# Up projection of a hybrid encoder step: the A11·B11 product of the first four column pairs taken ahead of the sets, and all 16 pairs by seven products

## The chip, the core and the metric

One core of a Trainium2 chip runs the whole kernel as one launch. The metric is the device time in microseconds of one execution. TensorE is PE in the profile (PEld is its weight load), VectorE is DVE, ScalarE is ACT, GpSimd is POOL, and SyncE, which issues nearly all transfers, is SP.

## What is computed

The reference is one encoder layer over 1056 columns (1024 prompt frames and 32 sample frames), with D_MODEL 1024 and D_FF 4096. The change lies in the first matrix product of the MLP:

```python
x = x + merged @ w_o
f = jnp.square(jax.nn.relu(rmsnorm(x, g_ffn) @ w_up)) @ w_down
x = x + f
```

Everything is fp32. Each operand is split into a high and a low part (fp32r), and a product of two operands takes three matmuls: high·high, high·low, low·high.

## The kernel before, in words

**Stages.** Input projection, attention and convolution, output projection (`w_o`, until 769 us of the span), up projection (769 to 1101 us), down projection (1101 to 1428 us), gate and final norm. Activations are held transposed: features in partitions, the 1056 columns along the free axis, in two halves of 528 and four quarters of 264.

**Up projection.** The 32 column blocks of `w_up` are taken as 16 pairs, `u0` to `u15`. With the two blocks of a pair as rows, and even and odd k blocks as columns, a pair is a 2x2 block product: A11, A12, A21, A22 (weights) times B11, B21 (first half of the columns) and B12, B22 (second half). One "product" over a quarter is 4 k blocks x 3 matmuls of 128x264, that is 12 matmuls (`products`). Pair `u0` is made plainly (`up_plain`): 8 products over two quarters each, 192 matmuls. Pairs `u1` to `u15` are made by seven products instead of eight (`seven`), with sums of weights S1 to S4 and sums of operands T1 to T4: 168 matmuls each. Between the products, PSUM results are moved and combined: `p1` (A11·B11), `s5` and `u2` are copied to SBUF by ACT, and four combinations with them are made by DVE.

**Weights of a pair.** `fetch_up` loads the two blocks (512 KB each) into `wraw`, which has four buffers. `prepare` is a generator that makes the sums on POOL (`s3`, `a21`, `s2`, `s4`, in that order, four instructions), then splits A11 and A12 with `load_w` (a cast to `whi` by ACT and a subtraction to `wlo` by DVE, 128x1024), and S1, S2, S3, S4, A22 with `half_w` (a cast `sh` by ACT and a subtraction `sl` by DVE, 128x512). Its argument `at` says after how many steps each of these is issued. `whi` and `wlo` come from a pool with two buffers each; `sh` and `sl` have four each:

```python
wsp = ctx.enter_context(tc.tile_pool(name="wsp", bufs=2))
...
hi = wsp.tile([P, kb, P], F32R, tag="whi", name=f"whi_{name}")
lo = wsp.tile([P, kb, P], F32R, tag="wlo", name=f"wlo_{name}")
nc.scalar.copy(hi, raw)
nc.vector.tensor_tensor(lo, raw, hi.bitcast(F32), op=ALU.subtract)
```

**What sets the order.** The instructions of PE, DVE, ACT and POOL stand in each engine's queue in the order in which the code issues them. `run(body)` steps through one generator, such as `seven`, which yields after each product over a quarter, and after each step it advances every generator in the list `side` by one: `prepare` of the next pair, `all_t` (splits of T1 to T4, two instructions for each of 16 tiles), loads, and `mean_squares` (three small products and eight reciprocals on DVE). SP's transfers stand in one queue of their own.

**End of the output projection.** `wo_post` adds the last result into the residual, `operands(7)` splits B22 and B21 of the last feature block, ACT squares it (`sq7`) and DVE adds that to `ssq1`. `prepare_plain("u0", 0)` stands inside the last round, `prepare_plain("u0", 1)` behind the first matmuls of `up_plain`.

**End of a pair.** After the A22 product over the first quarter, `mid_sums` makes three sums on DVE (`ta`, `m1`, `ta`, 128x528); after the second quarter ACT takes relu and square, and DVE makes a fourth sum (`tb`). All go to DRAM for the down projection.

Of the kernel before, what the change touches and what calls it, by code (L numbers as in the profile page):

```python
# [48 lines left out]
def tile_step(  # L49
# [129 lines left out]
    def prepare(s_, at=(6, 8, 10, 12, 14, 18)):  # L179
# [17 lines left out]
        }  # L197
        parts = [partial(part, k, x) for k, x in (("S1", a21), ("S2", s2), ("S3", s3), ("S4", s4), ("A22", a22))]
        for n, g in zip(at, [first] + parts):
            steps.setdefault(n, []).append(g)  # L200
        for n in range(max(at) + 1):
            for f in steps.get(n, ()):
                f()  # L203
# [18 lines left out]
    def seven(s_, m1, m2, last, after=None):  # L222


        after = after or {}
        w = ws.pop(s_)
        p1, u2, s5 = (
            [wpool[0].tile([P, TQ], F32, tag=k, name=f"{k}_{s_}{t}") for t in range(2)] for k in ("p1", "u2", "s5")
        )
# [9 lines left out]
        for t, a, b in q:  # L239
            x[t] = product("A11", "B11", t)  # L240
            nc.scalar.copy(p1[t], x[t])
            yield
        for t, a, b in q:
            z[t] = product("S1", "T1", t)
            nc.scalar.copy(s5[t], z[t])
            yield
        for t, a, b in q:
            product("S2", "T2", t, x[t])
            nc.scalar.copy(u2[t], x[t])
            yield  # L250
        for t, a, b in q:
            dve(m1[:, a], product("A12", "B21", t), p1[t], op=add)
            yield
        done("11")
# [1062 lines left out]
    def operands(n):  # L1317

        g = gffn[:, n : n + 1]
        by_half = list(zip(halves, ("B21", "B22") if n % 2 else ("B11", "B12")))  # L1320
        for c, k in by_half[::-1] if n == KD - 1 else by_half:
            d, src = operand(k, n // 2), x1[n][:, c]
            nc.scalar.activation(d[:, 0, :], src, AF.Copy, scale=g)
# [77 lines left out]
    def output_projection():  # L1401

        for n in range(KD):
            if n + 2 < KD:
                wo_fetch(n + 2)
            else:
                fetch_up(n + 2 - KD)
            if n + 1 < KD:
                wo_high(n + 1)
            else:  # L1410
                prepare_plain("u0", 0)
            if n == 0:
                branch_post(("a", KD - 1), 2)
                for t in range(NTT):
# [66 lines left out]
    def up_plain():
        w = ws["u0"]
        m = blk("m1_0"), blk("m2_0")
        terms, p_ = ((w["A11"], "B12"), (w["A12"], "B22")), []
        for t in range(2):
            p_.append(products(f"up01{t}", terms, quarters[t], ks=range(3), last=False))
        prepare_plain("u0", 1)
        for c, i in ((1, 0), (1, 1), (0, 0), (0, 1)):
            for t in range(2):
                a, b = (("A11", "A12"), ("A21", "A22"))[i]  # L1490
                terms = ((w[a], f"B1{c + 1}"), (w[b], f"B2{c + 1}"))
                if (c, i) == (1, 0):
                    ps = products("", terms, quarters[t], p_[t], ks=[3], first=False)
# [4 lines left out]
            square(m[i], halves[c])
            if (i, c) != (0, 1):
                nc.sync.dma_start(md(f"B{i + 1}{c + 1}", 0), m[i][:, halves[c]])  # L1500
        side.append(after(3, mid_sums(0, *m)))
# [408 lines left out]
    with tc.manual_schedule(engines=MM):  # L1910
# [10 lines left out]

        for j in range(KD // 2 - 1):
            fetch_t(j, 0)
        side += [prepare("u1", AT1), all_t(), after(3, call(fetch_up, 2))]
        run(up_plain())
        x1.clear()
        side.append(after(14, mean_squares()))
        for s_ in range(1, NSET):
            if s_ + 1 < NSET:
                side.append(prepare(f"u{s_ + 1}"))  # L1930
            if s_ + 2 < NSET:
                side.append(after(5, call(fetch_up, s_ + 2)))
            if s_ == NSET - 1:
# [161 lines left out]
```

## Time and profile before

| | |
|---|---|
| median of 3 runs | 1541.33 us (1541.09 to 1541.75) |
| profiled execution | 1542.94 us, span 1541.1 us |
| PE busy | 1522.7 us (99%) |
| DVE busy | 1056.5 us (69%) |
| ACT busy | 747.3 us (48%) |
| POOL busy | 335.1 us (22%) |
| HBM read, written | 186.31 MB, 80.72 MB |
| mean granted PE clock | 0.997 |

The span runs from the first to the last recorded instruction; the profiled execution took 1.8 us more than its span. In timeline rows the columns are start, duration, engine, line, operation, output<-input, count, and in brackets the idle time before it with what ended it. A range such as 278/284/293 is the shortest, the median and the longest of a group in ns.

### The profile page before, as it was taken

To read this page: it belongs to the slowest core of one execution; us is meant where nothing else is said; L and a number is where in the kernel's file an instruction comes from. 1 tells how busy PE (TensorE), PEld (TensorE's weight loads), DVE (VectorE), ACT (ScalarE), POOL (GpSimd) and SP (SyncE) were. 2 spreads that over 40 slices of the span, in tenths; PEclk is the share of its full clock that TensorE was granted. 3 is DMA by queue.
4 is the path that set the end of the run, shared out by engine and by line. 5 is a ranking of instruction groups with operands and counts; after the bars stand their busy time and mean duration, and the time that the engine had idled before them with its cause. 6 is when DMAs were issued, how large, how long until landed. Compare 5 with 4: busy or idle time off the path is not lost. (4 is left out here: it accounts for less than half of the span.)

```text
span 1541.1 us, 29464 instructions
## 1 busy us (share of the span) xinstructions
PE 1522.7 (99%) x11840; PEld 1511.4 (98%) x11840; DVE 1056.5 (69%) x1425; ACT 747.3 (48%) x1367; POOL 335.1 (22%) x342
## 2 busy tenths in 40 slices
PE   8999999999999999999999999999999999999997
PEld 8999999999999999999999999999999999999997
DVE  7568656656777887665577555445577986789756
ACT  6544444434555664322365555555643334434654
POOL 2123322230222232101312222222020220000253
PEclk9999999999999999999999999999999999999999
DMA  6513545415644843354354343444886897683443
GB/s 221 202 53 111 192 153 193 166 45 182 197 117 151 281 141 133 133 180 176 121 188 152 140 154 137 142 148 154 290 289 199 286 326 237 210 273 122 138 129 117
DMA packets 110569, 268.96 MB, mean 175 GB/s; under 512 B 12992, under 2 KB 30144, under 8 KB 110432
## 3 DMA queue, kind: packets, MB, share of 16 engines
q1 hardware_dynamic: 110144, 266.75, 51.2%
q8 instruction: 93, 1.52, 0.4%
q14 instruction: 44, 0.36, 0.1%
q10 hardware_dynamic: 288, 0.32, 0.1%
HBM read 186.31 MB, written 80.72 MB: 173 GB/s over the span
## 5 line engine op out<-in xcount | busy, mean ns | idle before, releaser
L1690 PE MATMUL ps_dn<-fh,whi_dn 128*128 128x264 f32 x896 | 254.7, 284 | 0.0
L1691 PE MATMUL ps_dn<-fl,whi_dn 128*128 128x264 f32 x896 | 254.5, 284 | 0.0
L1692 PE MATMUL ps_dn<-fh,wlo_dn 128*128 128x264 f32 x896 | 254.5, 284 | 0.0
L1692 PEld LDWEIGHTS ps_dn<-fh,wlo_dn 128*128 128x128 f32 x896 | 168.7, 188 | 0.0
L1691 PEld LDWEIGHTS ps_dn<-fl,whi_dn 128*128 128x128 f32 x896 | 168.5, 188 | 0.0
L1690 PEld LDWEIGHTS ps_dn<-fh,whi_dn 128*128 128x128 f32 x896 | 168.5, 188 | 0.0
L809 DVE TENSOR_TENSOR_SCAN r<-r 128x128 f32<-128x128 f32 (+3 forms) x64 | 86.6, 1353 | 5.6 <-POOL r L802 5.6
L203 POOL TENSOR_TENSOR s_i<-raw_i,raw_i 128x512 f32<-128x512 f32 x30 | 41.2, 1372 | 223.7 <-DVE slS_i L166 194.0
L203 POOL TENSOR_TENSOR s_u<-raw_u,raw_u 128x512 f32<-128x512 f32 x30 | 44.1, 1471 | 184.6 <-DVE slS_u L166 184.4
L1577 ACT CAST whi_dn<-raw_dn 128x1024 fp32r<-128x1024 f32 x40 | 42.1, 1051 | 84.7 <-PE ps_dn L1691 84.7
L802 POOL TENSOR_SCALAR_AFFINE_SELECT r<-r 128x128 f32<-128x128 f32 x64 | 40.1, 627 | 192.1 <-ACT r L795 192.1
L1583 DVE TENSOR_TENSOR wlo_dn<-raw_dn,whi_dn 128x1024 fp32r<-128x1024 f32 x40 | 61.3, 1531 | 28.5 <-ACT whi_dn L1577 28.5
L1774 POOL TENSOR_TENSOR xx<-xx,pgs 128x384 f32<-128x384 f32 (+1 forms) x23 | 24.3, 1058 | 216.4 <-DVE pgs L1773 209.8
L1603 DVE TENSOR_TENSOR fl<-mr,fh 128x1056 fp32r<-128x1056 f32 x56 | 70.0, 1249 | 0.3 <-ACT q L1643 0.3
L849 DVE TENSOR_TENSOR at<-pa,at 128x512 fp32r<-128x512 f32 (+2 forms) x96 | 51.9, 550 | 24.7 <-ACT at L848 24.2
L216 PE MATMUL ps_A11u<-T,shS_u 128*128 128x264 f32 x240 | 68.4, 285 | 0.0
L218 PE MATMUL ps_A11i<-T,slS_i 128*128 128x264 f32 x240 | 68.4, 285 | 0.0
L217 PE MATMUL ps_A11u<-T,shS_u 128*128 128x264 f32 x240 | 68.3, 285 | 0.0
L216 PE MATMUL ps_A11i<-T,shS_i 128*128 128x264 f32 x240 | 68.3, 285 | 0.0
L217 PE MATMUL ps_A11i<-T,shS_i 128*128 128x264 f32 x240 | 68.2, 284 | 0.0
L218 PE MATMUL ps_A11u<-T,slS_u 128*128 128x264 f32 x240 | 68.0, 283 | 0.0
L166 DVE TENSOR_TENSOR slS_i<-s_i,shS_i 128x512 fp32r<-128x512 f32 x45 | 36.1, 806 | 45.4 <-ACT shS_i L164 45.1
(451 smaller groups left out, 5607.8 us busy)
## 6 DMA issues: line engine op xcount, KB each, us to landing
raw_dn<-in_w_down_dram SPq DMA_DIRECT2D x56, 512.0 KB, 4.6
raw_i<-in_w_in_dram SPq DMA_DIRECT2D x34, 512.0 KB, 4.5
mr<-mdT SPq DMA_DIRECT2D x32, 528.0 KB, 5.7
raw_u<-in_w_up_dram SPq DMA_DIRECT2D x32, 512.0 KB, 3.6
mdB<-m SPq DMA_DIRECT2D x48, 264.0 KB, 2.4
mr<-mdB SPq DMA_DIRECT2D x24, 528.0 KB, 6.4
raw_pg<-in_w_ple_gate_dram SPq DMA_DIRECT2D x17, 512.0 KB, 3.6
mdT<-ta SPq DMA_DIRECT2D x32, 264.0 KB, 2.1
```

The source lines that it names most:

```text
L203: f()
L216: nc.tensor.matmul(p_, wh[:, k, :], o[:, 0, c], start=new and n == 0, stop=False, **on)
L217: nc.tensor.matmul(p_, wh[:, k, :], o[:, 1, c], start=False, stop=False, **on)
L218: nc.tensor.matmul(p_, wl[:, k, :], o[:, 0, c], start=False, stop=z, **on)
L809: nc.vector.tensor_tensor_scan(rev, rev, rev, 1.0, ALU.mult, ALU.bypass)
L849: nc.vector.tensor_tensor(al, pt[:, :nb, :], ah.bitcast(F32), op=ALU.subtract)
L1577: nc.scalar.copy(hi, dws[u])
L1583: dve(lo, raw, hi.bitcast(F32), op=sub)
L1603: dve(l, mraw.pop(v), opd[v].bitcast(F32), op=sub)
L1690: nc.tensor.matmul(ps, hi[:, j, :], oh, start=j == 0, stop=False)
L1691: nc.tensor.matmul(ps, hi[:, j, :], ol, start=False, stop=False)
L1692: nc.tensor.matmul(ps, lo[:, j, :], oh, start=False, stop=j == NP_ - 1)
```

## The change

The A11·B11 product of pairs `u0` to `u3` (`P` in the code) is made first, in `up_early`, and kept in SBUF (`held_p`, tiles `pe0` and `pe2`); the A12·B21 product (`C`) is added to it in the same PSUM buffer, and relu and square of that go to DRAM as B11 of the down projection. Each early pair needs one weight block only (`early_fetch`, `early_split`; names `eu0` to `eu3`). `up_plain` is gone. All 16 pairs then run through `up_set`. For the four held ones `seven` makes five products over two quarters (S1, S2, S3, S4, A22; 120 matmuls), and DVE adds or subtracts the held `p1` where `p1` used to be left in PSUM. Both weight blocks of these pairs are loaded (again for the first block) and prepared as before, without the A11, A12 split. The first half of `m1` is read back from DRAM for the sums. B12 is no longer split, as plain pairs alone used it.

```diff
-AT1 = (5, 4, 6, 7, 8, 12)
+AT1 = (5, 4, 6, 8, 10, 12)
+NEARLY = 4
+AT2 = (4, 6, 8, 10, 12, 15)
...
-            steps.setdefault(n, []).append(g)
+            if g is not first or s_ not in held_p:
+                steps.setdefault(n, []).append(g)
...
+    def early_split(s_):
+        early_w[s_] = even_odd(load_w(None, 0, KD, f"e{s_}", raw=early_raw.pop(s_)))
+
+    def early_first(s_, t):
+        p_ = early_ps[s_, t] = products(f"e{s_}_{t}", ((early_w[s_][0], "B11"),), quarters[t])
+        nc.scalar.copy(held_p[s_][:, quarters[t]], p_)
+
+    def early_second(s_, t):
+        p_ = early_ps.pop((s_, t))
+        products("", ((early_w[s_][1], "B21"),), quarters[t], p_)
+        return p_
...
+        if s_ in held_p:
+            p1 = [held_p[s_][:, quarters[t]] for t in range(2)]
+            for t, a, b in q:
+                z[t] = product("S1", "T1", t)
+                dve(s5[t], z[t], p1[t], op=sub)
+                yield
+            for t, a, b in q:
+                x[t] = product("S2", "T2", t)
+                dve(u2[t], x[t], p1[t], op=add)
+                yield
+        else:
...
             product("A22", "T4", t, x[t])
-            last(m2, a, x[t])
+            if s_ in held_p:
+                dve(m2[:, a], x[t], p1[t], op=add)
+                last(m2, a)
+            else:
+                last(m2, a, x[t])
...
-                fetch_up(n + 2 - KD)
+                early_up(n + 2 - KD)
...
-                prepare_plain("u0", 0)
+                early_split("u0")
...
+        order = [("P", 0), ("P", 1), ("C", 0), ("P", 2), ("C", 1), ("P", 3), ("C", 2), ("C", 3)]
+        for k, i in order:
...
+                if k == "P":
+                    early_first(s_, t)
+                    if t == 0 and i + 1 < NEARLY:
+                        early_split(f"u{i + 1}")
...
+                    p_ = early_second(s_, t)
+                    relu2(c11[i], quarters[t], p_)
                 yield
+            if k == "C":
+                nc.scalar.square(c11[i], c11[i])
+                nc.sync.dma_start(md("B11", i), c11.pop(i))
...
+        if s_ < NEARLY:
+            nc.sync.dma_start(m1[:, halves[0]], md("B11", s_))
...
-        side += [prepare("u1", AT1), all_t(), after(3, call(fetch_up, 2))]
-        run(up_plain())
+        early_up(2)
+        early_up(3)
+        side += [all_t(), after(1, call(fetch_up, 0)), after(3, prepare("u0", AT1)), after(7, call(fetch_up, 1))]
+        run(up_early())
...
-        for s_ in range(1, NSET):
+        for s_ in range(NSET):
             if s_ + 1 < NSET:
-                side.append(prepare(f"u{s_ + 1}"))
+                side.append(prepare(f"u{s_ + 1}", AT2) if s_ + 1 < NEARLY else prepare(f"u{s_ + 1}"))
```

How the order moves on ACT, from the squares of the output projection's last two blocks onward. Before (`whi_u0_1` is the second block of pair `u0`, `B22_3` and `B21_3` are the last operands):

```order
L1392 ACTIVATE sq6_9359<-xr6_9010 128x1056
L107 CAST whi_u0_1_9477<-raw_u0_1_9214 128x1024
L1323 ACTIVATE B22_3_9416<-xr7_9116,vecT_98 128x528
L1323 ACTIVATE B21_3_9419<-xr7_9116,vecT_98 128x528
L1392 ACTIVATE sq7_9422<-xr7_9116 128x1056
L1462 ACTIVATE m1_0_9437<-ps_up010_9439 128x264
```

On the same engine at the same place, now (`ps_eu0_0` is P of pair 0 over the first quarter, `whi_eu1` the cast that P of pair 1 reads, `whi_eu2` that of pair 2):

```order
L1360 ACTIVATE B21_3_9400<-xr7_9110,vecT_98 128x528
L1360 ACTIVATE B22_3_9403<-xr7_9110,vecT_98 128x528
L1432 ACTIVATE sq7_9406<-xr7_9110 128x1056
L220 COPY pe0_9425<-ps_eu0_0_9427 128x264
L109 CAST whi_eu1_9441<-raw_eu1_9307 128x1024
L1371 ACTIVATE xr6_9004<-xr6_9004,vecT_98 128x528
L220 COPY pe0_9425<-ps_eu0_1_9451 128x264
L161 CAST T1_3_9465<-w_3_9445 128x528
L220 COPY pe0_9425<-ps_eu1_0_9472 128x264
L109 CAST whi_eu2_9486<-raw_eu2_9421 128x1024
```

The cast of the second weight block stood ahead of the last operands and now stands behind them, the square and a copy out of PSUM.

On DVE, at the end of one pair by seven products and the start of the next. Before, from the S4 combination of `u1` on (`slS` is the low part of a weight sum, `rs2` belongs to `mean_squares`):

```order
L262 TENSOR_TENSOR m1_1_9718<-u2_u11_9723,ps_S1u1_1_9790 128x264
L166 TENSOR_TENSOR slS3_u2_9982<-s3_u2_9751,shS3_u2_9980 128x512
L1471 TENSOR_TENSOR ta1_9984<-m1_1_9718 128x528
L1473 TENSOR_TENSOR m1_1_9718<-m2_1_9719,m1_1_9718 128x528
L1475 TENSOR_TENSOR ta1_9984<-m1_1_9718 128x528
L1478 TENSOR_TENSOR tb1_9985<-m2_1_9719,ta1_9984 128x528
L1445 TENSOR_SCALAR rs2_10031<-ps_ms0_10032 128x352
L166 TENSOR_TENSOR slS4_u2_10037<-s4_u2_9752,shS4_u2_10035 128x512
L1445 TENSOR_SCALAR rs2_10031<-ps_ms352_10072 128x352
L1445 TENSOR_SCALAR rs2_10031<-ps_ms704_10104 128x352
L166 TENSOR_TENSOR slA22_u2_10109<-raw_u2_1_9572,shA22_u2_10107 128x512
L252 TENSOR_TENSOR m1_2_10009<-ps_A12u2_0_10128,p1_u20_10011 128x264
```

On DVE at the same place, now: from the A22 combination of `u0` over its first quarter on (`ps_S2u0_0` is the PSUM buffer in which it ends, `pe0` the held product, `ps_S1u1` and `ps_S2u1` the first products of the next pair):

```order
L301 TENSOR_TENSOR m2_0_9761<-ps_S2u0_0_9803,pe0_9425 128x264
L168 TENSOR_TENSOR slS2_u1_9914<-s2_u1_9784,shS2_u1_9912 128x512
L1511 TENSOR_TENSOR ta0_9916<-m1_0_9760 128x528
L1513 TENSOR_TENSOR m1_0_9760<-m2_0_9761,m1_0_9760 128x528
L1515 TENSOR_TENSOR ta0_9916<-m1_0_9760 128x528
L301 TENSOR_TENSOR m2_0_9761<-ps_S2u0_1_9818,pe0_9425 128x264
L1518 TENSOR_TENSOR tb0_9917<-m2_0_9761,ta0_9916 128x528
L264 TENSOR_TENSOR s5_u10_9947<-ps_S1u1_0_9949,pe0_9425 128x264
L168 TENSOR_TENSOR slS3_u1_9965<-s3_u1_9785,shS3_u1_9963 128x512
L264 TENSOR_TENSOR s5_u11_9948<-ps_S1u1_1_9971,pe0_9425 128x264
L268 TENSOR_TENSOR u2_u10_9945<-ps_S2u1_0_9986,pe0_9425 128x264
```

Between the fourth sum `tb` and the first instruction that takes a product of the next pair out of PSUM (L252) there stood five instructions of other work, and that instruction belonged to the next pair's fourth product. Now the first product's combination (L264) stands right behind `tb`, and the combination that frees the buffer of S2 (L268, `u2_u10`) stands three rows further. The A22 combination (L301), which ACT made before, stands ahead of and behind the three sums.

More of the change, by code (lines that the diff above doesn't have):

```diff
@@ L204, in prepare, with early_fetch @@
             yield
+    held_p, c11 = {}, {}
+    early_raw, early_w = {}, {}
+    def early_fetch(s_, w, n):
+        early_raw[s_] = raw_w(w, n, KD, f"e{s_}")
+    def early_split(s_):
[7 more added lines that the diff above has]
+        return p_
+    early_ps = {}
     def products(name, terms, c, p_=None, ks=range(4), first=None, last=True):
@@ L226, in seven @@
         w = ws.pop(s_)
-        p1, u2, s5 = (
-            [wpool[0].tile([P, TQ], F32, tag=k, name=f"{k}_{s_}{t}") for t in range(2)] for k in ("p1", "u2", "s5")
-        )
+        u2, s5 = ([wpool[0].tile([P, TQ], F32, tag=k, name=f"{k}_{s_}{t}") for t in range(2)] for k in ("u2", "s5"))
         q = [(t, quarters[t], quarters[2 + t]) for t in range(2)]
@@ L237, in done @@
             after.get(k, int)()
[L239 to L254, printed above, removed]
+        if s_ in held_p:
[9 more added lines that the diff above has]
+        else:
+            p1 = [wpool[0].tile([P, TQ], F32, tag="p1", name=f"p1_{s_}{t}") for t in range(2)]
+            for t, a, b in q:
+                x[t] = product("A11", "B11", t)
+                nc.scalar.copy(p1[t], x[t])
+                yield
+            for t, a, b in q:
+                z[t] = product("S1", "T1", t)
+                nc.scalar.copy(s5[t], z[t])
+                yield
+            for t, a, b in q:
+                product("S2", "T2", t, x[t])
+                nc.scalar.copy(u2[t], x[t])
+                yield
+            for t, a, b in q:
+                dve(m1[:, a], product("A12", "B21", t), p1[t], op=add)
+                yield
+            done("11")
         for t, a, b in q:
@@ L270, in seven @@
                 done("near")
+        held_p.pop(s_, None)
         done("21")
@@ L1319, in operands @@
         g = gffn[:, n : n + 1]
-        by_half = list(zip(halves, ("B21", "B22") if n % 2 else ("B11", "B12")))
-        for c, k in by_half[::-1] if n == KD - 1 else by_half:
+        for c, k in zip(halves, ("B21", "B22") if n % 2 else ("B11",)):
             d, src = operand(k, n // 2), x1[n][:, c]
@@ L1354, in fetch_up, with early_up @@
         fetch_pair(f"u{s_}", w_up, 2 * s_)
+    def early_up(s_):
+        early_fetch(f"u{s_}", w_up, 2 * s_)
     wo, xs = {}, {}
@@ L1479, in mid_sums, with up_early @@
         nc.sync.dma_start(md("T4", s_), tb[:, 0, :])
[L1481 to L1488, printed above, removed]
+    def up_early():
+        order = [("P", 0), ("P", 1), ("C", 0), ("P", 2), ("C", 1), ("P", 3), ("C", 2), ("C", 3)]
+        for k, i in order:
+            s_ = f"u{i}"
+            if k == "P":
+                if i % 2 == 0:
+                    pair, out = (blk(f"{c}{i}", F32, [P, 2, TH]) for c in ("pe", "ce"))
+                held_p[s_], c11[i] = pair[:, i % 2, :], out[:, i % 2, :]
             for t in range(2):
[L1490 to L1493, printed above, removed]
-                else:
-                    ps = products(f"up{i}{c}{t}", terms, quarters[t])
-                relu2(m[i], quarters[2 * c + t], ps)
+                if k == "P":
+                    early_first(s_, t)
+                    if t == 0 and i + 1 < NEARLY:
+                        early_split(f"u{i + 1}")
+                else:
+                    p_ = early_second(s_, t)
+                    relu2(c11[i], quarters[t], p_)
                 yield
[L1498 to L1501, printed above, removed]
+            if k == "C":
+                nc.scalar.square(c11[i], c11[i])
+                nc.sync.dma_start(md("B11", i), c11.pop(i))
     def up_set(s_):
         m1, m2 = blk(f"m1_{s_}"), blk(f"m2_{s_}")
+        if s_ < NEARLY:
+            nc.sync.dma_start(m1[:, halves[0]], md("B11", s_))
         sums_ = mid_sums(s_, m1, m2)
```

## The prediction

> **What bounds the kernel now.** I read the page's busy times first, then PE's list of waits, then busy time by stage.
>
> ```profile
> PE 1522.7 (99%) x11840; PEld 1511.4 (98%) x11840; DVE 1056.5 (69%) x1425; ACT 747.3 (48%) x1367; POOL 335.1 (22%) x342
> PE ps_g L216 <- ACT B L342: 6.1, 1, 6.1
> PE zf L752 <- ACT r L795: 1.0, 1, 1.0
> 768.50:792.20 23.70, 23.70 (x197) 23.70 (x196) 13.68 (x18) 13.40 (x24) 1.12 (x1) 1.00 0.46 155
> 833.00:1090.00 257.00, 257.00 (x2116) 257.00 (x2115) 136.54 (x205) 138.17 (x268) 65.97 (x48) 1.00 0.43 149
> ```
>
> PE is the bound. Its longest wait is 6.1 us, at the start; no other is over 1.0 us. In the stretch that the change rewrites (768.5 to 792.2, the plain pair, and the pairs after it) PE is busy for the whole of it: 23.70 of 23.70 us and 257.00 of 257.00 us. So each matmul taken away here is time gained, and each new wait of PE is time lost, one for one. The granted clock is 1.00 there.
>
> **What it removes: 24 matmuls.** Before: 192 + 15 x 168 = 2712. Now: 4 x 48 early, 4 x 120 for the held pairs, 12 x 168 for the others, 2688.
>
> ```profile
> 768.67 0.28 PE L216 MATMUL ps_up<-B,whi_u 128*128 128x264 f32 x1
> 792.06 0.29 PE L216 MATMUL ps_A11u<-B,whi_u 128*128 128x264 f32 x1
> ```
>
> The first matmul of the plain pair starts at 768.67, the first behind its 192 at 792.06: 23.39 / 192 = 0.1218 us each, 1.46 us for a product of 12. The 24 are worth **-2.9 us**. A measurement of this kernel can tell about 0.2% (3.1 us) from no change, so even the whole gain lies at that edge.
>
> **What it adds, 1: three waits for early weights.** The last operands and the plain pair's second block ran so:
>
> ```profile
> 768.71 1.05 ACT L107 CAST whi_u<-raw_u 128x1024 fp32r<-128x1024 f32 x1 [6.47 <-PE ps_wo L1380]
> 769.67 1.36 ACT L1323 ACTIVATE B<-xr,vecT 128x528 fp32r<-128x528 f32 x2
> 770.93 1.07 ACT L1392 ACTIVATE sq<-xr 128x1056 f32<-128x1056 f32 x1
> 773.97 0.39 ACT L1462 ACTIVATE m<-ps_up 128x264 f32<-128x264 f32 x1 [1.97 <-PE ps_up L218]
> 768.87 0.52 DVE L1384 TENSOR_TENSOR xr<-ps_wo,xr 128x352 f32<-128x352 f32 x1 [3.36 <-PE ps_wo L1381]
> 769.80 1.23 DVE L108 TENSOR_TENSOR wlo_u<-raw_u,whi_u 128x1024 fp32r<-128x1024 f32 x1 [0.40 <-ACT whi_u L107]
> 772.30 1.25 DVE L1394 TENSOR_TENSOR ssq<-ssq,sq 128x1056 f32<-128x1056 f32 x1
> ```
>
> P of pair 0 starts at 768.67 as the plain pair did: B11 and its weights are ready. It ends 24 matmuls later, at 771.6. P of pair 1 needs the cast of `eu1`, which now stands behind B21 and B22, the square and the copy. They start when DVE's last addition is done (769.4): 1.36 + 1.07 + 0.3 (the 0.39 of the copy, overlapped) bring ACT to 772.0, the cast takes 1.05, to 773.05. DVE adds the square into `ssq1` from 771.85 to 773.1 and then makes `wlo` in 1.23, to 774.3. The first low-weight matmul of P1 is its third, due at 771.85: PE waits **2.5 us**.
>
> P of pair 2 follows C of pair 0 directly, and `whi` and `wlo` have two buffers: the cast of `eu2` needs the one that C of pair 0 reads to its end. A cast starts as soon as the last reader is done: the row at 768.71 shows that, released by PE. So nothing covers 1.05 + 1.23, less the two matmuls that need only `whi` (0.24), plus some 0.1 in handing over: **2.2 us**. The same for P of pair 3 behind C of pair 1, **2.2 us**. ACT's and DVE's queues behind the two blocked splits hold the copies out of PSUM and T1 to T4; they have the next 48 matmuls (5.8 us) to catch up, for about eight ACT operations no longer than the cast, and later I find no wait from them.
>
> One of these may be longer. The second block of `u0` is loaded when `wlo_eu1` has freed its buffer (774.3), and lands 3.6 us later by the median row; POOL then runs its four sums about when `wlo_eu2` runs (781).
>
> ```profile
> raw_u<-in_w_up_dram SPq DMA_DIRECT2D x32, 512.0 KB, 3.6
> L1583 DVE TENSOR_TENSOR wlo_dn<-raw_dn,whi_dn x40: 1214/1225/2358, 1098.4 to 1420.7; 128x1024 fp32r<-128x1024 f32 x40
> ```
>
> The same operation elsewhere takes 1.2 us at the median and 2.36 at most, so this wait is 2.2 to 3.3; I take 2.5, near the median row. Sum of the early waits: **+7.2 us** (6.9 to 8).
>
> Other transfers: four more weight blocks, four reads of `m1`. SP stands at the loads of `u1` until POOL's s4 of `u0` is done (near 785: loaded at 778, then four instructions like the POOL rows below), with the T3 and T4 loads behind it; ACT comes to T3 some eleven operations behind the cast of `eu3` (788), near 794, which leaves them some 8 us. Were they late, the wait would be the lateness. The four dropped B12 splits lay beside other work: nothing.
>
> **What it adds, 2: a longer chain from held pair to held pair.** S3 accumulates into the buffer of S2, so it must wait for `u2` (L268), which DVE now makes. Before, the copy by ACT had the two quarters of A12 as cover; that product is gone. And L268 stands behind the end of the pair before: the low part of S2, three sums, L301, ACT's relu and square, `tb`, `s5`, the low part of S3, `s5`. The pieces, from the same place in a later pair:
>
> ```profile
> L252 DVE TENSOR_TENSOR m<-ps_A12u,p_u x30: 422/428/433, 805.0 to 1092.5; 128x264 f32<-128x264 f32 x30
> 835.66 0.61 ACT L164 CAST shS_u<-s_u 128x512 fp32r<-128x512 f32 x1
> 836.17 0.39 ACT L1462 ACTIVATE m<-ps_A11u 128x264 f32<-128x264 f32 x1
> 836.59 0.65 ACT L1465 ACTIVATE m<-m 128x528 f32<-128x528 f32 x1
> L166 DVE TENSOR_TENSOR slS_u<-s_u,shS_u x45: 631/693/1782, 790.3 to 1084.1; 128x512 fp32r<-128x512 f32 x45
> 837.07 0.69 DVE L1471 TENSOR_TENSOR ta<-m 128x528 f32<-128x528 f32 x1
> 837.80 1.68 DVE L1473 TENSOR_TENSOR m<-m,m 128x528 f32<-128x528 f32 x1
> 839.52 0.71 DVE L1475 TENSOR_TENSOR ta<-m 128x528 f32<-128x528 f32 x1
> 837.29 1.63 POOL L203 TENSOR_TENSOR s_u<-raw_u,raw_u 128x512 f32<-128x512 f32 x1 [0.69 <-DVE slS_u L166]
> ```
>
> From the end of A22's first quarter: L301 0.43, relu 0.39, cast of S2 0.61, its low part 0.69, sums 3 x 0.7, L301 0.43, relu 0.39, square 0.65, `tb` 0.7, `s5` 0.43, low part of S3 0.69, `s5` 0.43, `u2` 0.43: 8.4 us (rows start up to 0.09 before the end of the row before on one engine and 0.05 after it on another, which nearly cancel). PE's work in that time is A22's second quarter, S1 and S2: five products over a quarter, 7.3 us. PE waits 1.1 us before S3.
>
> POOL makes it longer. The second sum at 837.80 took 1.68 instead of 0.7, ending 0.56 after POOL's own instruction. Now POOL's first two sums for the pair after next start when the low part of S2 is done, one right behind the other, exactly beside the three sums. Rows with two POOL instructions in a row:
>
> ```profile
> 754.51 1.64 POOL L203 TENSOR_TENSOR s_u<-raw_u,raw_u 128x512 f32<-128x512 f32 x1
> 756.23 1.65 POOL L203 TENSOR_TENSOR s_u<-s_u,raw_u 128x512 f32<-128x512 f32 x1
> 755.03 1.68 DVE L155 SCALAR_TENSOR_TENSOR xr<-xr,vecT,xr 128x528 f32<-128x528 f32 x1
> 756.64 1.80 DVE L155 SCALAR_TENSOR_TENSOR xr<-xr,vecT,w 128x528 f32<-128x528 f32 x1
> L1449 DVE RECIPROCAL rs<-rs x8: 923/970/972, 825.8 to 840.1; 128x132 f32<-128x132 f32 x8
> ```
>
> Two DVE instructions then take about 1 us more each: +1.9. So each of the three transitions (u0 to u1, u1 to u2, u2 to u3) costs PE 3.0 us; without POOL's part 1.1. The eight reciprocals, 0.97 us each, fall into `u2`, two of them between `tb` and `u2`'s L268: 3.0 + 1.9 = 4.9 us there; a third delays L301 at the end of `u2` by some 0.8: 3.8 us into `u3`. Sum 3.0 + 4.9 + 3.8 = 11.7. At the start, ACT's cast of A22 of `u0` waits for S1 to be finished with its buffer, and DVE has that low part, T4 and two `s5` ahead of its first L268: 0.3 to 2 us, I take 1. Into `u4`, an ordinary pair, POOL is idle beside the sums and S2 comes two products later: nothing. **+12.7 us** (5.5 without POOL's part, 15 with some more of it).
>
> **The sum.** -2.9 + 7.2 + 12.7 = +17.0 us. Against the profiled span that is 1558.1; that execution took 1542.94 us, 0.1% above the median of the runs, 1541.33. On the median: **1558 us**, 1551 to 1563 by the ends above.
>
> **The rivals.**
>
> *The early waits only.* If DVE keeps ahead in the held pairs (as it does in every pair now, where PE shows no wait), there is 7.2 - 2.9 = +4.3: 1545.6. For it: DVE is at 69%. Against it: the chain is made of waits one behind the other, not of load. 16 in 100.
>
> *The clock falls as well.* After a long wait PE may restart slowly. The start of the kernel shows what that is:
>
> ```profile
> 7.73 0.42 PE L218 MATMUL ps_g<-B,wlo_i 128*128 128x264 f32 x1
> 13.23 0.32 PE L216 MATMUL ps_g<-B,whi_i 128*128 128x264 f32 x1
> ```
>
> Behind the wait of 6.1 us, 25 matmuls lie between these two, 0.22 us apart instead of 0.12: 2.5 us lost in one such phase. The longest wait forecast is 4.9 us, and two more are over 3; one to three phases give 1561 to 1566. The granted clock at the waits of up to 1.0 us stayed at 1.00, so nothing in this trace tells at what length it begins. 14 in 100. [...]
>
> *The other side: the waits are covered, and only the 24 matmuls count.* Place: P of pairs 1 to 3. If ACT and DVE had the parts ready before PE arrives, 1541.3 - 2.9 = 1538.4, just within 0.2%. It decides at 2.3 us of cover between the last reader of a `whi` buffer and the next P; the order in `up_early` leaves none, so only a third buffer or other work on PE would do it. 8 in 100. That the change doesn't do what it says is no likelier: the order shows the 120 matmuls of a held pair.
>
> **How the numbers follow.** The forecast has 62 in 100. The range reaches from the first rival (1545.5) to the far end of the second (1566), leaving out the third and a rest. Faster by over 0.2% needs the third rival and a little more: 0.04. Within 0.2%: the rest of it and the smallest waits of the first, 0.06. Slower by over 0.2%: 0.90.
>
> **What would show it.** In the changed profile: PE waits for the `wlo` of the early weights (L110), three times, 2.2 to 3.3 us each; PE waits for DVE's L268 before S3 of `u1`, `u2`, `u3`, the second the longest; beside the three sums two DVE rows of 1.7 us with POOL rows of 1.6; 24 fewer matmuls at the same pace. Wrong if PE's waits from 769 to 870 us sum to less than 12 us or more than 25, or if they stand at loads or elsewhere.

## The result, and the profile after

The changed kernel takes **1566.82 us** (median of 5 runs, 1564.83 to 1567.86) against 1541.75 us (1541.09 to 1542.73) for the kernel before on the same chip: a ratio of 1.0157, 95% interval 1.0145 to 1.0168. It is slower by 25 us. The direction and the mechanism were forecast; the forecast of 1558 us is 9 us short, and the median lies 0.8 us above the upper end of the range. The profiled execution took 1565.93 us, its span is 1564.2 us, its mean granted clock 0.993.

The busy times of the page show the 24 matmuls that are gone (11816 instead of 11840) and PE "busy" for 6.8 us longer all the same: the same work, partly at a lower pace.

```profile
PE 1529.5 (98%) x11816; PEld 1516.0 (97%) x11816; DVE 1070.3 (68%) x1447; ACT 743.0 (48%) x1358; POOL 341.2 (22%) x346
```

PE's list of waits from 760 to 1110 us names the two sets of waits that were forecast (columns: total, count, longest):

```profile
PE ps_S2u L239 <- DVE u_u L268: 10.2, 4, 3.9
PE ps_eu L241 <- DVE wlo_eu L110: 3.0, 3, 1.6
PE ps_eu L239 <- ACT whi_eu L109: 2.9, 3, 1.0
PE ps_A11u L241 <- DVE slS_u L168: 0.2, 1, 0.2
```

16.3 us of waits stand where there were none. L268 is `u2` ahead of S3, L110 and L109 are the parts of the early weights. `u4`'s own wait (last row) is 0.2 us; nothing was forecast there.

The busy time by stage (PE, PEld, DVE, ACT, POOL, then the granted clock) shows where it happens, and a second thing:

```profile
768.50:800.00 31.50, 25.55 (x186) 24.27 (x186) 24.79 (x27) 20.45 (x40) 10.48 (x7) 0.95 0.57 205
820.00:840.00 20.00, 17.10 (x119) 16.13 (x118) 13.42 (x23) 6.64 (x12) 5.34 (x5) 0.91 0.45 148
840.00:860.00 20.00, 16.11 (x114) 15.94 (x113) 16.10 (x26) 6.53 (x12) 3.82 (x4) 0.83 0.40 134
880.00:1120.00 240.00, 239.76 (x1965) 239.33 (x1964) 127.00 (x191) 132.68 (x252) 61.50 (x44) 1.00 0.45 157
```

From 880 us on PE is busy throughout again. But between 768 and 860 us the clock is as low as 0.95, 0.91 and 0.83. Timeline rows of PE behind the longest wait show what that is:

```profile
847.01 0.56 PE L239 MATMUL ps_S2u<-T,shS_u 128*128 128x264 f32 x1 [3.88 <-DVE u_u L268]
847.37 0.42 PE L240 MATMUL ps_S2u<-T,shS_u 128*128 128x264 f32 x1
...
851.99 0.38 PE L240 MATMUL ps_S2u<-T,shS_u 128*128 128x264 f32 x1
852.20 0.28 PE L241 MATMUL ps_S2u<-T,slS_u 128*128 128x264 f32 x1
```

The matmuls start 0.22 us apart (847.37 to 847.59 and so on) until 852.2, then 0.12 again: 22 matmuls at the low pace. The granted clock says the same:

```profile
845.40:852.10 6.70, 5.09 (x23) 5.12 (x24) 5.43 (x9) 0.00 (x0) 2.54 (x2) 0.50 0.28 85
```

It is 0.50 also from 824.9 to 828.2 (11 matmuls at the low pace, behind the wait that ends at 824.9) and from 790.8 to 794.1 (14, behind the two waits at P3), 47 matmuls in all, and stays at 1.00 behind the wait of 3.3 us at 867. At 0.098 us more each they cost 4.6 us.

The end of pair 0 on DVE, and POOL at the same time:

```profile
817.52 1.68 DVE L1513 TENSOR_TENSOR m<-m,m 128x528 f32<-128x528 f32 x1
819.23 1.68 DVE L1515 TENSOR_TENSOR ta<-m 128x528 f32<-128x528 f32 x1
824.33 0.42 DVE L268 TENSOR_TENSOR u_u<-ps_S2u,pe 128x264 f32<-128x264 f32 x1
```

```profile
817.00 1.63 POOL L206 TENSOR_TENSOR s_u<-raw_u,raw_u 128x512 f32<-128x512 f32 x1 [13.65 <-DVE slS_u L168]
818.71 1.63 POOL L206 TENSOR_TENSOR raw_u<-raw_u 128x512 f32<-128x512 f32 x1
```

Two of the three sums take 1.68 us, each ending 0.6 us behind a POOL instruction. L268 ends at 824.75, and PE's wait of 2.9 us ends at 824.90. The step was forecast in these terms.

From start to start of the matmuls, less the ordinary 0.122 each, the early waits come to 1.95 (P1), 2.9 (P2) and 2.4 us (P3), 7.2 in all; those before S3 to 0.3, 3.3, 4.3 and 3.4 us, 11.4; `u4` 0.4; the 47 slow matmuls 4.6; the first matmuls behind each wait, at 0.23 us, 1.0. With -2.9 that is 21.7 us, and the first matmul of the down projection starts 21.85 us later than before (1122.86 instead of 1101.01). The span grew by 23.1; the last 1.3 us build up slowly behind that point, mainly from 1123 to 1233 us (0.7) and from 1324 to 1380 us (0.4), without a wait of PE that was not there before, and their cause stays open.

### The profile page after: what moved, and what is told of

Read it like the earlier page. It is cut to its first block, busy times and chain, and to the rows that moved or that the text cites. A ratio compares the mean times of both kernels' runs of the same rounds, so it can differ in the third digit from the quotient of the medians.

```text
span 1564.2 us, 29485 instructions
## 1 busy us (share of the span) xinstructions
PE 1529.5 (98%) x11816; PEld 1516.0 (97%) x11816; DVE 1070.3 (68%) x1447; ACT 743.0 (48%) x1358; POOL 341.2 (22%) x346
## 4 chain that ended last, share of the span: by engine, by line
PE 92%; DVE 5%; ACT 2%; issue 1%; DMA 0%; SPq 0%; DVEq 0%; ACTq 0%
PE ps_dn L1732 7%; PE ps_dn L1734 7%; PE ps_dn L1733 7%; PE ps_A11i L241 3%; PE ps_A11i L239 3%; PE ps_A11i L240 3%; PE ps_A11u L241 3%; PE ps_A11u L239 3%; PE ps_A11u L240 3%; PE av L904 2%; PE ps_pg L118 2%; PE ps_wo L1421 2%; PE ps_wo L1420 2%; PE ps_wo L1419 2%; PE ps_pg L120 2%; PE ps_pg L119 2%
## 5 line engine op out<-in xcount | busy, mean ns | idle before, releaser
L1502 ACT ACTIVATE m<-m 128x528 f32<-128x528 f32 (+1 forms) x52 | 31.8, 611 | 98.7 <-DVE m L290 37.6
L1421 PE MATMUL ps_wo<-mh,wlo_wo 128*128 128x352 f32 x192 | 62.2, 324 | 0.0
L1420 PE MATMUL ps_wo<-ml,whi_wo 128*128 128x352 f32 x192 | 62.1, 323 | 0.0
```

The source lines that it names most:

```text
L1420: nc.tensor.matmul(ps, hi[:, k, :], ml[k][:, c], start=False, stop=False, skip_group_check=True)
L1421: nc.tensor.matmul(ps, lo[:, k, :], mh[k][:, c], start=False, stop=k == KD - 1, skip_group_check=True)
```

## The experiments

The theory: a wait for free weight buffers at the early products, a chain from held pair to held pair on DVE that POOL makes longer, and a clock that falls in the waits. The rival: DVE has too much work for what PE does meanwhile, so that mending one wait brings the next.

| run | median, us | ratio to before (95%) | PE's waits, 760 to 1110 us | matmuls in slow phases |
|---|---|---|---|---|
| changed kernel | 1566.8 | 1.0157 (1.0145 to 1.0168) | 16.3 | 47 |
| buffers of their own | 1565.6 | 1.0150 (1.0131 to 1.0168) | 17.2 | 62 |
| late sums | 1561.9 | 1.0125 (1.0109 to 1.0140) | 13.8 | 29 |
| changed kernel again | 1569.2 | 1.0175 (1.0160 to 1.0190) | 15.9 | 99 |
| no POOL sums, pairs 2 to 4 | 1563.5 | 1.0137 (1.0121 to 1.0152) | 13.3 | 70 |
| mean squares later | 1566.0 | 1.0148 (1.0126 to 1.0170) | 15.0 | 30 |
| late sums, mean squares later | 1564.7 | 1.0144 (1.0127 to 1.0161) | 12.5 | 29 |
| buffers, no POOL sums, pairs 0 and 1 | 1556.8 | 1.0092 (1.0077 to 1.0107) | 11.3 | 23 |
| filled waits | 1564.1 | 1.0137 (1.0122 to 1.0153) | 7.1 | 31 |
| all remedies | 1553.5 | 1.0075 (1.0061 to 1.0089) | 8.4 | 16 |
| sums on DVE as well | 1553.6 | 1.0076 (1.0064 to 1.0089) | 8.4 | 15 |
| tuned | 1553.3 | 1.0069 (1.0056 to 1.0083) | 9.3 | 15 |
| tuned again | 1553.1 | 1.0068 (1.0055 to 1.0082) | 8.7 | 0 |

The last two columns are of the one profiled execution. The executions of one kernel differ by up to 8 us here, those of the kernel before by under 3. With the mean squares later they reach from 1561.2 us at a mean granted clock of 0.996 to 1569.4 us at 0.991, and 0.005 of the span is 7.8 us, nearly the whole difference. The profiled execution is the shortest of its four in both runs with the mean squares later (1561.2 and 1560.0), and the longest in the changed kernel again (1571.8). So the steps below are read from the traces first.

**Buffers of their own for pairs 2 and 3** (the P halves go into tiles that only the pairs use later).

```diff
+    def split_p(s_):
+        for i in range(2):
+            src = raw[:, 4 * i : 4 * i + 4 : 2, :]
+            h, l = (wpool[0].tile([P, 2, P], F32R, tag=k, ...) for k in ("u2", "s5"))
...
-                    if t == 0 and i + 1 < NEARLY:
-                        early_split(f"u{i + 1}")
+                    if t == 0 and i == 1:
+                        split_p("u2")
```

> The first halves of the early weights of pairs 2 and 3 are split into tiles of their own (four small tiles that the pairs only use later), so their casts no longer wait for the second products of pairs 0 and 1. If the early waits are waits for a free weight buffer: the waits of P2 and P3 (2.9 and 2.3 us beyond the ordinary pace in the changed kernel's trace) go, and with them the 14 matmuls at 0.22 us behind P3 (1.4 us): 6.6 us less than the changed kernel's 1566.8, so 1560. If ACT and DVE are too busy there to make the parts in time whatever the buffers, each wait stays at 1.5 us or more: 1563 to 1565, and the waiting rows name the cast or the low part with ACT or DVE busy just before.

The wait at P2 is gone, but the time is the same within the intervals: 1565.6 us. PE's list of waits (L291 is `u2`'s line here, `es_u` the low part for P3):

```profile
PE ps_S2u L262 <- DVE u_u L291: 13.3, 4, 4.0
PE ps_eu L264 <- DVE es_u L232: 2.0, 1, 2.0
```

The wait at P3 is 2.0 us again, now for DVE's low part, and pair 0's S3 waits 3.1 us instead of 0.2 (the first row now holds four long waits). DVE ran these at the time:

```profile
782.03 1.79 DVE L162 TENSOR_TENSOR T<-rt,T 128x528 fp32r<-128x528 f32 x1
783.75 1.78 DVE L110 TENSOR_TENSOR wlo_cu<-raw_eu,whi_cu 128x512 fp32r<-128x512 f32 x1
785.45 0.70 DVE L162 TENSOR_TENSOR T<-rt,T 128x528 fp32r<-128x528 f32 x1
```

A low part that takes 0.70 us at 785.45 took 1.8 twice before it, beside POOL's sums for pair 0. The busy time of 768.5 to 805 us, before (first) and in this run (second):

```profile
768.50:805.00 36.50, 36.50 (x301) 36.50 (x300) 25.42 (x32) 22.08 (x43) 6.18 (x4) 1.00 0.53 181
```

```profile
768.50:805.00 36.50, 29.80 (x239) 28.96 (x238) 31.79 (x40) 24.53 (x51) 12.68 (x8) 1.00 0.58 198
```

DVE has 31.8 us of work in these 36.5 us, where before it had 25.4, and POOL works 12.7 us beside it instead of 6.2. Ahead of P3's low part DVE has no idle time from 777.35 us on: this wait is DVE's load. Ahead of pair 0's S3 DVE stands idle for 4.0 us, for ACT's casts of T operands, and two of these wait for their loads. SP's queue, in which the loads stand, had waited for POOL's last sum until 785.0 us:

```profile
SPq L100 <- POOL s_u L206: 11.4, 1, 11.4
```

So POOL's sums can make pair 0 late in two ways, by what they add to DVE and by the loads that they hold up. The waits for buffers in the changed kernel had covered a queue that was late anyway. The expectation of 1560 fell; the rival's 1563 to 1565 is nearer, but it held only for P3.

**Buffers, and POOL's sums of pairs 0 and 1 left out.**

```diff
+        bare = s_ in ("u0", "u1")
+        if bare:
+            s2, s3, s4 = a11, a11, a12
-        steps = {
+        steps = {} if bare else {
```

The splits of these pairs then take parts of the raw weights, so the run is no version to use and only prices the sums.

> As in the run with buffers of their own for pairs 2 and 3, and with GpSimd's sums of the weights of pairs 0 and 1 left out (the splits take parts of the raw weights in their place). In that run the waits moved to the low part at P3 (2.3 us) and to L268 of pair 0 (3.4 us), with low parts of 1.8 us on VectorE beside GpSimd's sums. If VectorE's load, lengthened by GpSimd, bounds the stage from the early products to pair 0: its low parts take 0.7 us and those two waits go, 5 to 6 us less than 1565.6, 1559 to 1561. If the loads of T1 to T4 or ACT's casts bound it: 0 to 2 us less, 1564 to 1566.

1556.8 us: 8.8 less than with the buffers alone. The row of the same stretch, and PE's waits:

```profile
768.50:805.00 36.50, 34.59 (x279) 33.75 (x278) 26.14 (x43) 25.64 (x54) 2.65 (x3) 1.00 0.62 214
```

```profile
PE ps_S2u L265 <- DVE u_u L294: 9.4, 4, 4.0
PE ps_eu L265 <- ACT whi_eu L109: 0.9, 1, 0.9
PE ps_eu L267 <- DVE wlo_eu L110: 0.8, 1, 0.8
```

DVE's load fell by 5.7 us with no instruction of its own taken away, and PE's work in the stretch rose from 29.8 to 34.6 us. At the early products only P1's wait is left (1.7 us in the last two rows), and pair 0's S3 waits 0.2. So POOL's sums are the price of the early stage once the buffers are free: at P3 by what they add to DVE; at pair 0's S3 no run tells that from the loads of T operands, the last of which is issued at 784.8 us here instead of 789.1. That this went further than the 5 to 6 us expected fits the clock: 23 slow matmuls instead of 62, another 3.8 us.

**No POOL sums for pairs 2, 3 and 4** (the same edit with other names, on the changed kernel).

> GpSimd's sums of the weights of pairs 2, 3 and 4 are left out (the splits take parts of the raw weights in their place), so that nothing runs on GpSimd beside VectorE's three sums at the ends of pairs 0, 1 and 2. If GpSimd lengthens VectorE's chain as forecast (1.9 us of 3.0 at each of three transitions): the sums take 0.7 us each, the waits before S3 fall by 1.9 us each, 5.7 us, and the slow matmuls behind them by 1 to 3 us: 7 to 9 less, 1558 to 1560. If the chain is bound by ACT or by the low parts instead: within 1.5 us of 1566.8.

PE's waits (L271 is `u2`'s line here) and the end of pair 0 on DVE:

```profile
PE ps_S2u L242 <- DVE u_u L271: 4.4, 4, 2.0
PE ps_A11u L242 <- ACT shS_u L166: 3.0, 1, 3.0
```

```profile
819.38 0.71 DVE L1516 TENSOR_TENSOR m<-m,m 128x528 f32<-128x528 f32 x1
824.26 0.43 DVE L271 TENSOR_TENSOR u_u<-ps_S2u,pe 128x264 f32<-128x264 f32 x1
```

The second sum (L1516) takes 0.71 us instead of 1.68, and the third the same. The waits before S3 of pairs 1 to 3 fell from 10.5 to 4.7 us from start to start (without the slow matmuls behind them), 1.9 each, as forecast; and what is left at pair 1 is 1.1 us, the 1.1 that the chain gave without POOL. The time fell by 3.3 us only, and not by the 7 to 9 expected: a wait of 3.0 us for ACT's cast stands at pair 4, and this execution has 70 slow matmuls.

**The mean squares later.**

```diff
-        side.append(after(14, mean_squares()))
+        side.append(after(60, mean_squares()))
```

> The mean squares (three matmuls, three evictions and eight reciprocals of 0.97 us on VectorE) start 60 steps behind the early products instead of 14, in an ordinary pair. By the chain, only the two reciprocals between tb and L268 of pair 2 and the one ahead of L301 at its end are on the path: the waits before S3 of pairs 2 and 3 fall by 1.2 to 1.8 and 0.6 to 0.8 us: 2 to 2.5 us less, 1564 to 1565. If VectorE's load as a whole sets the pace of the held pairs, all eight count: 5 to 8 us less, 1559 to 1562.

PE's rows at S3 of pairs 1, 2 and 3:

```profile
823.94 0.36 PE L239 MATMUL ps_S2u<-T,shS_u 128*128 128x264 f32 x1 [2.90 <-DVE u_u L268]
...
841.76 0.36 PE L239 MATMUL ps_S2u<-T,shS_u 128*128 128x264 f32 x1 [2.90 <-DVE u_u L268]
...
859.62 0.36 PE L239 MATMUL ps_S2u<-T,shS_u 128*128 128x264 f32 x1 [2.90 <-DVE u_u L268]
```

Three equal waits, 3.07 us each from start to start, for which 3.0 had been forecast without the reciprocals. In the changed kernel the same three were 3.07, 4.04 and 3.43 us, so the reciprocals were worth 1.0 us at pair 2 (1.9 forecast) and 0.4 at pair 3 (0.8 forecast). The run without POOL sums, which keeps them, agrees: 1.0 and 0.4 us more there than at pair 1. By the waits the chain's reading holds and the load's 5 to 8 us does not. The medians don't show it, since the runs spread over 8 us; the profiled execution alone, at 1561.2 us, lies in the load's range, with 17 slow matmuls fewer.

**Late sums.** The four sums at the ends of pairs 0 to 2 are issued behind the next pair's L268, and `m1` is loaded behind their stores.

```diff
+            if s_ < NEARLY - 1:
+                side.append(after(3, call(list, sums_)))
+            else:
+                next(sums_, None)
```

> The four sums at the end of pairs 0, 1 and 2 stand on VectorE behind the next pair's two L268 instead of ahead of them; the load of m1 is moved behind the sums' stores. If the chain from pair to pair through the sums makes PE wait before S3: the three waits (3.3, 4.3 and 3.3 us beyond the ordinary pace) and the slow matmuls behind two of them (3.2 us) go, but for the reciprocals in pair 2 (up to 2 us): 12 to 14 us less, 1553 to 1555. If VectorE has simply too much work in the held pairs, the sums only move the wait to A22 or the next S3: 3 to 6 us less, 1561 to 1564.

1561.9 us, 5 less and not 12 to 14: inside the second case, 1561 to 1564. The first of PE's waits beside the early ones, and the row on DVE that carries the one for L290:

```profile
PE ps_S2u L241 <- DVE slA_u L168: 2.8, 2, 2.0
PE ps_S2u L239 <- DVE m L290: 1.7, 1, 1.7
PE ps_S2u L239 <- DVE u_u L268: 1.7, 2, 0.9
```

```profile
829.89 0.71 DVE L1518 TENSOR_TENSOR tb<-m,ta 128x528 f32<-128x528 f32 x1 [3.71 <-DMA mdT<-m]
```

The waits for L268 fell from 10.2 to 1.7 us, so the sums were what stood ahead of it. In their place come the low part of A22 and the S3 combination (L290), as the second case had it. At pair 1 the cause is a buffer: DVE stood still for 3.71 us at `tb`, whose buffer a store to DRAM still held, with all of the next pair's combinations queued behind it. The longest wait, 2.0 us at pair 2, has no such gap: DVE is busy without one from 839.80 us on, with five of the eight reciprocals and the late sums ahead of that low part. There the sums did only move the wait.

**Late sums with buffers taken earlier, and the mean squares later.**

```diff
         ta, tb = blk(f"ta{s_}", F32, [P, 2, TH]), blk(f"tb{s_}", F32, [P, 2, TH])
+        if s_ < NEARLY - 1:
+            yield
```

> As in the run with the late sums, but ta and tb take their buffers ahead of the next pair's m1 and m2 (in that run tb waited 3.7 us for a store to free one), and the mean squares start in an ordinary pair. If order alone makes the waits of pairs 1 to 3: at most 2 us of waits are left from S1 of pair 1 to pair 4, 1552 to 1555. If VectorE has too much to do for the 14.6 us of TensorE's work in a held pair: 5 us or more of waits stay, wherever they stand: 1558 to 1561.

1564.7 us, and the same row again:

```profile
828.35 0.71 DVE L1520 TENSOR_TENSOR tb<-m,ta 128x528 f32<-128x528 f32 x1 [3.71 <-DMA mdT<-m]
```

Taking the buffer earlier did not change which one it was. In pairs 1 to 4, 6.4 us of waits are left, 2.9 of them behind that buffer and 1.6 at pair 4. The expectation fell: both cases forecast less than 1564.7 us, and the waits that are left are over the 5 us of the load's case only with those behind the buffer. So the run does not tell order from load.

**Filled waits.** The first run with a fill in its text (e3_fill) has none in its program, because a later function of the same name takes its place; it is the changed kernel a second time and is used as that.

> TensorE runs 20 extra matmuls (2.4 us) ahead of S3 of pair 1 and 28 (3.4 us) ahead of S3 of pair 2, on an operand that is there, into a bank that nobody reads; they fit in the waits. If the matmuls at 0.22 us behind these waits are the clock that fell in the wait: they run at 0.12, 3.2 us less, 1563.6. If something else holds those matmuls back (weights or operands that come late): no change, 1566.8, with the 0.22 us rows still there.

It ran at 1569.2 us with nearly the same waits (15.9 us) and 99 slow matmuls instead of 47. PE's rows at the first slow phase and at the ends of two later ones:

```profile
773.98 0.51 PE L241 MATMUL ps_eu<-B,wlo_eu 128*128 128x264 f32 x1 [0.75 <-DVE wlo_eu L110]
...
777.56 0.29 PE L239 MATMUL ps_eu<-B,whi_eu 128*128 128x264 f32 x1
...
856.08 0.29 PE L241 MATMUL ps_S1u<-B,slS_u 128*128 128x264 f32 x1
...
876.45 0.32 PE L240 MATMUL ps_S1u<-B,shS_u 128*128 128x264 f32 x1
```

The first one begins behind two waits of 0.88 and 0.75 us at P1; in the other execution the waits there were 0.87 and 0.75 us, and the clock stayed at 1.00 (from 768.50 to 790.74 us). The phases shown end at 777.56, 856.08 and 876.45. The granted clock in this execution is 0.86 from 768.5 to 795 us, 0.89 to 809, 1.00 to 825, 0.92 to 847, 0.84 to 868 and 0.80 to 885; in the other one it is 0.94, 1.00, 1.00, 0.89, 0.88 and 1.00. Then the kernel with the fill:

```diff
                 dve(u2[t], x[t], p1[t], op=add)
+                if t == 1 and s_ in SPIN:
+                    spin(SPIN[s_])
...
+            nc.tensor.matmul(ps, d[:, 0, :P], d[:, 0, quarters[0]], start=True, stop=True)
```

> TensorE runs 22, 30 and 22 extra matmuls (2.7, 3.7 and 2.7 us) ahead of S3 of pairs 1, 2 and 3, on an operand that is there, into a bank that nobody reads; they fit in the waits (3.3, 4.3 and 3.3 us). In two traces of the changed program (the run called e3_fill turned out to be it without any fill) the matmuls behind these waits ran at 0.22 us for 3.3 and 5.7 us more than at the ordinary pace. If that is the clock that fell in the wait: those phases go, 3 to 6 us less than 1567 to 1569, 1562 to 1565. If something else holds these matmuls back: no change, and the rows at 0.22 us stay.

The busy time from 809 to 868 us, changed kernel first, filled second:

```profile
809.00:868.00 59.00, 48.94 (x358) 47.61 (x358) 42.70 (x66) 19.81 (x36) 16.14 (x11) 0.91 0.39 132
```

```profile
809.00:868.00 59.00, 57.84 (x461) 56.42 (x460) 44.03 (x69) 19.83 (x36) 17.49 (x12) 1.00 0.41 138
```

With 2.7 to 3.7 us of extra matmuls in the waits, the clock is 1.00 there instead of 0.91, and no slow phase follows S3; the two that are left (31 matmuls) lie behind the unfilled early waits. 1564.1 us: 2.7 less than the one measurement of the changed kernel, within the intervals of the two, and 5.1 less than the other. It is the clock: operands that come late would not come sooner for extra work.

**All remedies.** Buffers, the split of pair 1 ahead of the last operands, late sums with T4's sum in `m1` (no buffer to wait for), mean squares later.

```diff
         wo_post(KD - 1, 2)
+        early_split("u1")
         wo_after(KD - 1)
...
-        dve(tb[:, 0, :], m2[:, a], ta[:, 1, :], op=sub)
+        dve(m1[:, a], m2[:, a], ta[:, 1, :], op=sub)
```

> All remedies by order and by buffers together: weight tiles of their own for pairs 2 and 3, the split of pair 1 ahead of the last operands, the late sums (T4's sum now goes into m1's first half, which is no longer needed, so it waits for no buffer), the mean squares in an ordinary pair. If order and buffers make all the waits: 3 us or less are left from 768 to 900, 1542 to 1546. If VectorE's load bounds the stage from the early products to pair 0, the wait of pair 1 only moves as well: some 7 us of waits stay up to S3 of pair 0 and 3 in the pairs behind it, with one or two slow phases of 1.5 us: 1550 to 1554.

1553.5 us, within the second case. PE's waits:

```profile
PE ps_S2u L262 <- DVE u_u L291: 2.7, 3, 1.2
PE ps_eu L264 <- DVE es_u L232: 1.9, 1, 1.9
PE ps_eu L262 <- ACT eu_u L231: 1.7, 1, 1.7
PE ps_A11u L262 <- ACT shS_u L166: 1.4, 1, 1.4
```

P1's wait is gone, and P3's grew from 2.0 to 3.6 (rows 2 and 3): it moved, as a stage bound by load would have it. The waits of the held pairs are down to small ones of up to 1.2 us, 2.5 us in all in pairs 1 to 3.

**Sums of pairs 0 to 3 on DVE.**

```diff
+                (at[1], s3, a11, a21, sub), (at[1], a21, a21, a22, add), (at[2], s2, a21, a11, sub), (at[4], s4, s2, a12, sub)
+            ):
+                steps.setdefault(n, []).append(partial(dve, o, x, y, op=op))
```

> As the run with all remedies, and the sums of the weights of pairs 0 to 3 are made by VectorE instead of GpSimd (0.7 us each, at the step of the split that needs them), so that no low part stands beside a GpSimd sum. If GpSimd's lengthening of VectorE's low parts (1.1 us each, some eight of them up to pair 0) is the load that bounds the early stage: VectorE gains 4 to 6 us there net of its four sums of 2.8, and the waits up to S3 of pair 0 fall to 1 to 3 us: 1543 to 1548. If VectorE's own count of instructions bounds it: the same as the run with all remedies or up to 6 us slower.

1553.6 us, no change, which was the second case: P3's wait is 2.0 us and pair 0's S3 is nearly on time, but in the held pairs DVE now stands before low parts whose casts ACT can only begin when DVE's sum is done.

**Tuned.** Sums of pair 0 alone on DVE, a step earlier; A22's split ahead of the late sums; pair 4's splits earlier.

```diff
-AT2 = (4, 6, 8, 10, 12, 15)
+AT2 = (4, 6, 8, 10, 12, 13)
```

> As the run with all remedies; VectorE makes the weight sums of pair 0 alone, one step ahead of the splits that need them (GpSimd makes the others), the low part of A22 stands ahead of the four late sums, and pair 4 splits its weights two to three steps earlier. If VectorE's load up to pair 0 and the order behind it are what was left: the waits of 1.9 and 2.2 us at P3 fall to 1 or less together, that of 1.2 before S3 of pair 0 to 0.6, those of pair 4 (1.7 and 0.5) to 0.5, and no slow phase or one is left: 1544 to 1548. If ACT's or VectorE's queue only blocks elsewhere: 1550 to 1554 again.

1553.3 us. P3's waits fell to 0.4 us in PE's list, but pair 0 waits 2.1 and pair 4 waits 4.0 us for ACT, whose queue stands behind the earlier splits. Queues blocked elsewhere, as the second case had it.

**Tuned again.** Pair 4's steps as before, POOL's sums for pair 1 four steps later.

```diff
+        if s_ == "u1":
+            steps = {n + 4: g for n, g in steps.items()}
```

> As the run before it, but pair 4 splits its weights at its old steps, and GpSimd's sums for pair 1 start four steps later, behind pair 0's L268 (in the run before, they lengthened four of VectorE's low parts ahead of it by 3.5 us). If each remaining wait is one row's lateness: the wait of pair 0 falls from 2.1 to 0.6 us or less, that of pair 4 from 4.0 to 1.9, so 3.5 us less than 1553.3, and a slow phase fewer makes it 5: 1548 to 1550. If the work only stands late elsewhere (pair 1's splits): 1552 to 1554.

1553.1 us; pair 0's wait is still 2.1 us. POOL's first sum of pair 1, in the run before and in this one, and the low part of A22 on DVE here:

```profile
792.34 1.29 POOL L212 TENSOR_TENSOR s_u<-raw_u,raw_u 128x512 f32<-128x512 f32 x1 [29.82 <-DVE slS_u L168]
```

```profile
793.30 1.29 POOL L214 TENSOR_TENSOR s_u<-raw_u,raw_u 128x512 f32<-128x512 f32 x1 [29.83 <-DVE slS_u L168]
```

```profile
796.80 1.78 DVE L168 TENSOR_TENSOR slA_u<-raw_u,shA_u 128x512 fp32r<-128x512 f32 x1
```

POOL began at 793.30 instead of 792.34, and P of pair 0 starts as much later in this run (768.56 instead of 767.60): the four steps changed nothing. Nothing was queued ahead of the sums, so they started as soon as their buffer was free (released by a low part of DVE). Issuing later did not delay this idle engine. So A22's low part again takes 1.78 us.

No version beats the kernel before. The best four, at 1553, are 10 to 12 us behind it, with 8 to 9 us of waits.

## Why the prediction was right in kind and short in size

**The 24 matmuls: -2.9 us.** Right: 24 fewer at an unchanged 0.122 us where nothing waits.

**Early waits: +7.2.** Right in sum (7.2), with P1 0.55 us shorter, since one of the two operands ahead of its cast was made earlier than forecast, and P2 and P3 a little longer; P2's `wlo` is the one beside POOL's sums, as forecast. What the forecast did not see is that these waits also hid queues that were late anyway: without them the time stays.

**Held pairs: +12.7.** Measured 11.4, and 0.4 at `u4` where nothing was forecast. The parts were right one by one: 3.07 us for each transition without reciprocals (3.0 forecast), POOL's part 1.9 (1.9), the chain without POOL 1.1 at pair 1 (1.1). Pairs 2 and 3 were taken 0.9 and 0.4 us too long, by the waits alone: the reciprocals cost 1.0 us at pair 2 and not 1.9, and why was not followed. Two figures of the forecast do not follow from its terms: without POOL's part they give 7.0 us and not 5.5, and the ends, counted on the median throughout, give 1552 to 1561 us and not 1551 to 1563.

**The step that failed: the sum takes no term for the clock.** It stood as a rival at 14 in 100, "one to three phases" behind the waits over 3 us, instead of in the sum. Measured: 4.6 us in one execution and 9.7 in another (99 matmuls at 0.098 us), plus 1.0 us for the first matmul behind each wait. The reading that kept it out was wrong: the forecast says that the clock stayed at 1.00 at the waits of up to 1.0 us. That trace has a fall in mid-kernel, behind two short waits between 382 and 385 us:

```profile
382.62 0.30 PE L791 MATMUL z<-ks,q 128*128 128x128 f32 x1 [0.52 <-issue]
384.70 0.39 PE L791 MATMUL z<-ks,q 128*128 128x256 f32 x1 [0.89 <-ACT r L795]
385.44 0.42 PE L659 MATMUL ps_g<-B,whi_g 128*128 128x264 f32 x1
```

```profile
385.40:388.70 3.30, 3.30 (x16) 3.11 (x14) 1.86 (x4) 1.34 (x7) 0.87 (x4) 0.50 0.90 295
```

So the clock fell to 0.50 there behind two waits of 0.5 and 0.9 us, and the waits of 2.2 to 2.5 us forecast for the early products were candidates too. What decides whether it falls was not shown: in the changed kernel it stayed at 1.00 behind the waits of 0.87 and 0.75 us at P1 and of 1.01 and 1.55 us at P2, and fell to 0.50 behind those of 1.01 and 0.75 us at P3.

**Where the 9 us lie.** Up to the down projection the trace has 21.7 us where 17.0 were forecast: the clock and the first matmuls behind the waits add 5.6, and the shorter waits of the held pairs take 0.9 off. Behind it 1.3 us stay open. The other 2.5 us are executions: the profiled one of the kernel before is 1.6 us above the median that the forecast starts from, and that of the changed kernel 0.9 us below its own.

**"The chain is made of waits one behind the other, not of load."** Shown in the main for the held pairs, where leaving out POOL's sums took the waits for L268 from 10.2 to 4.4 us and all remedies left 2.5 us of waits in pairs 1 to 3. Wrong for the stretch up to pair 0: with the buffers DVE had 31.8 us of work there in 36.5, and the waits were 6.8 us. POOL's sums left out took them to 2.0 us. Order alone (pair 1's split earlier) left 4.5, and with pair 0's sums on DVE as well 2.3 to 2.6. The rival "only the 24 matmuls count" was said to turn on a third buffer or other work on PE; the run with the buffers shows that buffers would not have been enough.

The test set in advance (waits from 769 to 870 us between 12 and 25 us) gave 16.1 by the trace's list.

## What to carry to other kernels

When a change shortens the work of the engine that bounds a stage, set the other engines' work per unit against the new, shorter time, including what contention adds (5.7 of 31.8 us of DVE's work up to pair 0 here, with the buffers), before counting on their low share of the whole span. Price a new wait twice: by its length, and by the slow matmuls that may follow it (4.6 and 9.7 us in two executions here); several waits of 1 to 4 us in a row deserve a term in the sum and not a place among the rivals. And where a wait goes, look for the queue that it was hiding before counting the gain.

## What the hardware showed unexpectedly

- Slow phases behind short waits: matmuls 0.22 us apart instead of 0.12, 7 to 25 of them, behind waits of 2.9 and 3.9 us and behind pairs of waits of 0.9 and 0.75 us; in the same program 47 in one execution and 99 in another.
- A phase was 3.4 or 6.8 us long in the changed kernel: the granted clock is 0.50 from 790.74 to 794.15, from 824.87 to 828.29 and from 845.35 to 852.18 us, and 1.00 between these. It stayed at 1.00 behind the wait of 3.3 us that ends at 867.42, which cost its length alone.
- The DVE rows of 128x512 and 128x528 with two SBUF inputs that stand above beside a POOL instruction took 1.68 to 1.79 us instead of 0.70; those at 817.52 and 819.23 us start beside one and end 0.57 us behind it. In the run with the buffers POOL's sums of pairs 0 and 1 added 5.7 us to DVE's load in a stretch of 36.5 us (31.8 instead of 26.1).
